# Dense products first at half clock, single turns, `pr` as one padded product, five last sums open in PSUM, and the last squares summed in three pieces

## The chip, the cores and the metric

The kernel runs on one core of a Trainium2 chip. The metric is the device time of one execution in microseconds (us). A core has TensorE (PE in the rows, PEld its weight loads), VectorE (DVE), ScalarE (ACT), GpSimd (POOL) and SyncE (SP), which here issues the transfers. The engines run their own instruction streams in order and wait for each other by semaphores.

## The reference

One layer of a hybrid decoder for a prompt of 1024 tokens and eight sample tokens that share the weights; width 1024, all in fp32:

```python
xn = _rms_norm(x, p['norm_g'][l])
h = xn @ p['w_in'][l]
pool_v, pool_g, rw, rw_g, q, xa_g = jnp.split(h, IN_SPLITS, axis=-1)
pool_y = _pool_mix(...) * jax.nn.silu(pool_g)
...
rws = rw + (prev - rw) * p['shift_mu'][l]
rwkv_y, S_T = _rwkv7(rws, wkv[l], ...)          # 8 heads of 64, a scan over the tokens
rwkv_y = rwkv_y.astype(x.dtype) * jax.nn.silu(rw_g)
xa_y = _cross_attend(q, mem_k[l], mem_v[l]) * jax.nn.silu(xa_g)
mixed = jnp.concatenate([pool_y, rwkv_y, xa_y], axis=-1)
x = x + mixed @ p['w_out'][l]
...
y = _rms_norm(x, p['final_norm_g'])
```

In `_rwkv7` the key is divided by its norm in each head (`kk / max(sqrt(sum(kk*kk)), 1e-12)`), and each token updates a 64 x 64 state per head.

## The kernel before

The activations lie with features on the partitions and tokens along the row. The prompt is worked in two parts: part 0 is 512 prompt tokens and the eight sample tokens (520 columns, two chunks of 260), part 1 is 512. Every fp32 operand of a large product is split into a high and a low half (type fp32r), and a product of one k-tile is three products: high x high, high x low, low x high. So an output tile of 128 features takes 24 products for eight k-tiles: `pt` in the input projection, `pto` in the output projection (`mh`, `ml`, `mu` are halves of its input).

The RWKV branch is cut into eight units (four pairs of heads x two parts). A unit goes through `rwkv_prep` (1124; the key norm is in it: sums of squares `pn` on PE, an rsqrt in nine small DVE operations `rsq_y`/`rsq_t`, ACT spreads it to `rsb`, PE multiplies it back as `prs`, DVE makes `kk`), then `rwkv_solve` (1269; inverts the small triangular blocks; the result is X), then `rwkv_solved` (1335; `pr` = X times C), then `rwkv_chain` (1348; `pc`, `py` with `Wd` between them, chunk after chunk) and `rwkv_norm` (1397). In `pr` the two heads of a unit take 64 rows each, so a group of four chunks is eight products of 64 x 64 tiles of PE.

The end of the program is `second_part` (1761): the output projection of part 1. Seven of eight k-tiles are summed for all eight output tiles first; each sum goes to SBUF with the residual `xres` added (DVE, `y`). When the last unit's k-tile (number 5) is there, three last products per tile follow (`w5`), DVE adds the tile (`y<-pto,y`), ACT squares it, DVE adds the square into `yacc`; the last tile's squares go to PE alone. `last_norm` (1804) sums `yacc` and `ysq` over the partitions on PE (`pss`), makes `ms` and its rsqrt, spreads it (`pb`), scales the tiles and stores `out_y`. `out_norm` (1854) does the same for part 0, in the middle of the output projection of part 1.

What sets the order is a planner in the program (`Loom`, 118): every operation is recorded (`record`, 223, called from line 228, which is why nearly all rows have that line) in a stream (chains, solves, preps, norms, fills, out_norm, samples and so on), and `weave` (452) plays the engines forward with estimated costs and emits each engine's sequence. Who goes first is decided by tables: RANK (45) gives each stream two priorities, one on PE and one on the other engines; LINE (54) is the order of work items (`k3` is the key tile of unit 3, `o1` the output projection of part 1, `g`, `v`, `r`, `p`, `h`, `x` others); HELP (62) says which small operations go to POOL or ACT instead of DVE. In `choose` (434) the next PE operation is picked: when the planner takes the clock to be half, operations whose estimated time is at most DENSE go last:

```python
return (cold and o.passes * o.cost <= DENSE, x[0][0] + (STAY if o.tiling != now else 0), x[0][1])
```

## Time and profile before

| | us |
|---|---|
| three executions | 704.91, 707.35, 1009.45 (median 707.35) |
| profiled execution | 701.2, its span 699.4 |
| PE busy | 645.4 (92%) |
| DVE busy | 532.3 (76%) |
| ACT busy | 433.2 (62%) |
| POOL busy | 161.9 (23%) |
| mean granted PE clock | 0.957 |

The span is the time from the first to the last instruction. A granted clock of 1.00 is 2.4 GHz, 0.50 is 1.2 GHz. In a row of the timeline stand the start, the duration of the group, the engine, the line, the operation, result <- operands, the shape and the number of instructions; in brackets the idle time of the engine ahead of it and what ended it. Durations of PE products overlap, so the step from one start to the next is the time that a product takes from the stream. An fp32 product (not fp32r) appears as two instructions.

### The profile page before, as it was taken

What the parts mean: (1) busy time and instruction counts of PE and PEld (TensorE: products, weight loads), DVE (VectorE), ACT (ScalarE), POOL (GpSimd) and SP (SyncE); (2) the same over time, 40 slices, a digit from 0 to 9 for tenths busy, and PEclk for the clock granted to TensorE, in tenths of its full rate; (3) what the DMA queues carried; (4) which work ended last, traced back from release to release, by engine and by line L of the source; (5) the groups of instructions that cost most, each with busy time, mean ns of one, the idle gap of its engine ahead of it and who ended that gap; (6) DMA issues with size and microseconds to landing.
All of it is one profiled execution on the core that took longest, in us unless ns stands there. A gap on an engine that the chain in (4) does not pass through costs nothing.

```text
span 699.4 us, 15473 instructions
## 1 busy us (share of the span) xinstructions
PE 645.4 (92%) x5698; PEld 559.6 (80%) x5698; DVE 532.3 (76%) x1318; ACT 433.2 (62%) x1233; POOL 161.9 (23%) x192
## 2 busy tenths in 40 slices
PE   8989999889999999999999889979989999998993
PEld 7989899778899878878788768767767888996762
DVE  7687789878886999688999496997675785557454
ACT  9487465658569577984465336555678987753221
POOL 3242523330421023231300040024021001221301
PEclk9999999989999999999899999999998999999995
DMA  7347468462342515225355725617404524657733
GB/s 253 115 143 257 145 234 286 156 207 76 111 170 91 197 62 165 67 83 191 88 174 170 262 90 160 236 48 219 128 14 141 176 85 152 220 168 243 237 114 120
DMA packets 59427, 109.40 MB, mean 156 GB/s; under 512 B 11144, under 2 KB 20432, under 8 KB 59352
## 3 DMA queue, kind: packets, MB, share of 16 engines
q1 hardware_dynamic: 59352, 108.42, 47.1%
q8 instruction: 45, 0.74, 0.4%
q14 instruction: 30, 0.25, 0.1%
HBM read 75.37 MB, written 33.02 MB: 155 GB/s over the span
## 4 chain that ended last, share of the span: by engine, by line
PE 50%; DVE 28%; DMA 8%; ACT 7%; issue 4%; SPq 1%; POOL 1%; DVEq 0%; ACTq 0%; POOLq 0%
PE pt L228 19%; PE pto L228 10%; PE pg L228 3%; PE py L228 3%; DMA w<-in_win 3%; PE pf L228 2%; DVE y L228 2%; DVE w L228 2%; DVE prod L228 2%; DVE Z L228 2%; DVE BK L228 1%; PE pr L228 1%; PE pc L228 1%; DMA Z<-in_zinit 1%; PE pkv L228 1%
## 5 line engine op out<-in xcount | busy, mean ns | idle before, releaser
L228 PE MATMUL pt<-xh,w 128*128 128x260 f32 (+1 forms) x1104 | 285.1, 339 | 4.6 <-DVE w L228 2.0
L228 PEld LDWEIGHTS pt<-xh,w 128*128 128x128 f32 x1104 | 188.7, 193 | 22.1 <-DVE w L228 2.8
L228 PE MATMUL pt<-xl,w 128*128 128x260 f32 (+1 forms) x552 | 185.3, 336 | 0.0
L228 PEld LDWEIGHTS pt<-xl,w 128*128 128x128 f32 x552 | 106.3, 193 | 7.8 <-issue 0.6
L228 PE MATMUL pto<-mh,w 128*128 128x260 f32 (+1 forms) x320 | 74.4, 313 | 2.3 <-DVE y L228 2.1
L228 DVE TENSOR_TENSOR w<-w,w 128x512 fp32r<-128x512 f32 x80 | 58.9, 743 | 21.9 <-ACT w L228 17.7
L228 ACT ACTIVATE w<-w 128x512 fp32r<-128x512 f32 x96 | 58.3, 623 | 24.7 <-DMA w<-in_win 13.3
L228 PEld LDWEIGHTS pto<-mh,w 128*128 128x128 f32 x320 | 52.7, 189 | 8.1 <-DVE y L228 5.4
L228 PE MATMUL pto<-ml,w 128*128 128x260 f32 (+1 forms) x160 | 50.3, 314 | 0.0
L228 POOL TENSOR_TENSOR w<-w,w 128x512 fp32r<-128x512 f32 x16 | 26.7, 1667 | 80.8 <-ACT w L228 63.0
L228 ACT ACTIVATE SV<-py,PC 64x64 f32<-64x64 f32 x112 | 34.7, 309 | 17.1 <-PE py L228 15.3
L228 PE MATMUL py<-SV,E 128*128 128x64 f32 x256 | 38.2, 266 | 0.0
L228 PEld LDWEIGHTS py<-SV,E 128*128 128x128 f32 x256 | 35.6, 196 | 1.7 <-ACT Y L228 0.5
L228 ACT ACTIVATE Wd<-pc 64x64 f32<-64x64 f32 x128 | 27.7, 216 | 14.9 <-PE pc L228 13.2
L228 PE MATMUL pg<-E,BK 64*128 64x128 f32 x256 | 32.6, 304 | 3.7 <-DVE BK L228 3.1
L228 PEld LDWEIGHTS pg<-E,BK 64*128 64x128 f32 x256 | 27.5, 205 | 9.5 <-POOL BK L228 2.3
L228 PEld LDWEIGHTS pto<-ml,w 128*128 128x128 f32 x160 | 30.2, 189 | 1.1
L228 PE MATMUL pc<-SV,E 128*128 128x128 f32 x128 | 27.1, 294 | 3.5 <-ACT SV L228 3.3
L228 ACT ACTIVATE LX<-pg 32x256 f32<-32x256 f32 x64 | 20.5, 321 | 15.7 <-PE pg L228 14.5
L228 PE MATMUL pto<-mu,w 128*128 128x512 f32 x96 | 26.5, 420 | 2.3 <-DVE w L228 2.3
L228 PE MATMUL py<-Wd,C 128*128 128x128 f32 x128 | 27.2, 295 | 1.5 <-ACT Wd L228 1.5
L228 DVE TENSOR_TENSOR y<-pto,xres 128x260 f32<-128x260 f32 (+1 forms) x24 | 12.1, 511 | 21.4 <-PE pto L228 20.9
(354 smaller groups left out, 1442.6 us busy)
## 6 DMA issues: line engine op xcount, KB each, us to landing
w<-in_win SPq DMA_DIRECT2D x98, 256.0 KB, 3.7
ws<-w SPq DMA_DIRECT2D x34, 512.0 KB, 3.8
w<-ws SPq DMA_DIRECT2D x34, 512.0 KB, 4.0
out_y<-y SPq DMA_DIRECT2D x16, 256.0 KB, 2.1
xr<-in_xT SPq DMA_DIRECT2D x12, 256.0 KB, 3.3
xr<-in_xT SPq DMA_DIRECT2D x8, 260.0 KB, 4.4
mr<-mixd SPq DMA_DIRECT2D x8, 260.0 KB, 2.6
xres<-in_xT SPq DMA_DIRECT2D x8, 260.0 KB, 3.6
```

Of the source, the lines that this page charges most:

```text
L228: op = Op(eng, lambda: f(*a, **k), (x[1] if eng == "PE" else x[2], self.seq))
```

## The change

- The planner's tables: RANK has new numbers, LINE another order. The rule in `choose` now puts last the operations whose columns are at most 0.7 of their estimated time (RICH) when the planner takes the clock to be half; DENSE is not read any more. A new table NUDGE moves 238 single operations (named by stream and number) up or down in priority.
- A second queue of transfers on ACT (`out`, `aq`), and other engines for three operations of the chain (`helped("wm")` and so on): HELP names none of them, so nothing goes there. HELP names one new entry, `xr1`.
- `pr`: X is written into a lasting tile XB of 128 x 128 blocks whose off-diagonal quarters are zeroed once at the start. A group is four products with 128 rows instead of eight with 64; sixteen memsets of X go.
- `second_part`: output tiles 3 to 7 keep their sums in five PSUM banks. Their residual is split in two halves (`xr`, ACT and POOL) and added by two products with an identity (`identr`). The last products go on summing there. Tiles 0 to 2 are taken out and added as before. `w5` comes in four transfers at output tile 4. Squares read PSUM. The sums over partitions are twelve products of three pieces: `yacc` of tiles 0 to 5, then the squares of tile 6, then of tile 7.
- `last_norm`: tiles 3 to 7 are scaled out of PSUM into new tiles.

PE has 4232 products instead of 4282 (`pr` 64 instead of 128, `pss` with `ysq` 8 instead of 4, ten identity products); DVE has 11 operations fewer, ACT 6 more, POOL 10 fewer.

```diff
-LINE = ("v0 k3 o0 r3 x r6 g0 k1 v3 r4 k2 h1 p3 k4 k5 g1 r1 v5 g6 v1 k6 v6 p1 v2 v7 r5 k7 o1 r2 v4 p0 g7 h0 g3 "
-        "p2 g4 g5 r7 g2")
-DENSE = 112.0
+LINE = ("v0 k3 o0 r3 r6 k1 v3 p3 r4 k2 g0 h1 x g1 k4 k5 r1 g6 v5 v1 v2 v6 k6 p1 v7 r2 r5 o1 k7 p2 h0 v4 p0 g7 "
+        "g3 g4 g5 r7 g2")
+RICH = 0.7
+NUDGE = {
+    ('ahead_of_chain', 1, 151): -0.1, ('ahead_of_chain', 1, 158): -0.1, ('ahead_of_chain', 1, 159): 67.2,
...
+        key = (*x[7], n)
+        turn = (x[1] if eng == "PE" else x[2]) + NUDGE.get(key, 0.0)
...
-                return (cold and o.passes * o.cost <= DENSE, x[0][0] + (STAY if o.tiling != now else 0), x[0][1])
+                return (cold and o.columns <= RICH * o.passes * o.cost, x[0][0] + (STAY if o.tiling != now else 0), x[0][1])
...
-            po.memset(X[r1, :, 32:64], 0.0)
+            X = XB[:, :, r1.start:r1.start + 64]
...
-            for hr in (LO, HI):
-                pe.matmul(pr_[hr, 128 * c:128 * c + 128], X[hr, 4 * g + c, :], C[hr, c, :],
-                          start=True, stop=True)
+            pe.matmul(pr_[:, 128 * c:128 * c + 128], XB[:, 4 * g + c, :], C[:, c, :], start=True, stop=True)
...
+            if ft == 4:
+                w5 = []
+                for q in range(4):
...
+                    sy.dma_start(w5[q].bitcast(F32), wlast[:, 2 * q:2 * q + 2])
...
+            o = mmb("pto") if ft < 5 else fill("pto") if ft == 5 else sol("pto") if ft == 6 else wide("pto")
+            if ft >= 3:
+                xr = [rp.tile([P, HT], F32R, tag=t_, name="xr" + t_) for t_ in ("u4", "u5")]
+                split(xres, *xr, vp("xr", 1))
...
-            ve.tensor_tensor(y, o, xres, op=ALU.add)
-            Y.append(y)
+            if ft >= 3:
+                for x in xr:
+                    pe.matmul(o, identr, x, start=False, stop=False)
+                Y.append(o)
...
-            ve.tensor_tensor(y, o, y, op=ALU.add)
+            if ft < 3:
+                ve.tensor_tensor(y, o, y, op=ALU.add)
...
+            for j in range(4 if ft >= KT - 3 else 0):
+                pe.matmul(pss[:, j:j + 1], (acc if ft == KT - 3 else sq)[:, 128 * j:128 * j + 128], ones_c,
+                          start=(ft == KT - 3 and j == 0), stop=(ft == KT - 1 and j == 3))
...
-                ve.scalar_tensor_tensor(y, y, col(C_FG, ft), pb, op0=ALU.mult, op1=ALU.mult)
+                ve.scalar_tensor_tensor(y, o, col(C_FG, ft), pb if ft < 3 else rsy, op0=ALU.mult, op1=ALU.mult)
```

**Place A: PE, the last products.** Rows of the instruction order (line, operation, result <- operands, columns; the numbers behind a name are buffers). Before, `w_1505` is the last k-tile's weight, `mh_1493` and `ml_1494` its input; the sums over the partitions follow in pairs:

```order
L228 MATMUL pto<-ml_1494,w_1505 128x512
L228 MATMUL pto<-mh_1493,w_1505 128x512 x2
L228 MATMUL pto<-ml_1494,w_1505 128x512
L228 MATMUL pto<-mh_1493,w_1505 128x512
L228 MATMUL pss<-ones_c,yacc 128x1
L228 MATMUL pss<-ones_c,ysq 128x1
L228 MATMUL pss<-ones_c,yacc 128x1
L228 MATMUL pss<-ones_c,ysq 128x1
L228 MATMUL pss<-ones_c,yacc 128x1
L228 MATMUL pss<-ones_c,ysq 128x1
L228 MATMUL pss<-ones_c,yacc 128x1
```

After, with `w_1485` and `w_1486` two of the four pieces of that weight and `xru` the halves of a residual:

```order
L317 MATMUL pto<-mh_1498,w_1485 128x512
L317 MATMUL pto<-xru_1509,identr 128x512
L317 MATMUL pto<-xru_1510,identr 128x512
L317 MATMUL pto<-ml_1499,w_1485 128x512
L317 MATMUL pto<-mh_1498,w_1485 128x512 x2
L317 MATMUL pto<-ml_1499,w_1485 128x512
L317 MATMUL pto<-mh_1498,w_1485 128x512
L317 MATMUL pto<-mh_1498,w_1486 128x512
L317 MATMUL pto<-ml_1499,w_1486 128x512
L317 MATMUL pto<-mh_1498,w_1486 128x512 x2
L317 MATMUL pto<-ml_1499,w_1486 128x512
L317 MATMUL pto<-mh_1498,w_1486 128x512
```

Right behind them on PE, after (`pb` spreads the scale over the partitions):

```order
L317 MATMUL pss<-ones_c,yacc 128x1 x4
L317 MATMUL pss<-ones_c,ysq 128x1 x8
L317 MATMUL pb_1526<-con,rsq_y 128x128 x3
L317 MATMUL pb<-con,rsq_y 128x128 x4
L317 MATMUL pb_1526<-con,rsq_y 128x128
```

Two identity products stand among the last 24 products, and `pss` is four products of `yacc` and then eight of squares in one row.

**Place B: DVE and SP, out_norm of part 0** (`y<-y,cols,rsx` is the scaling of an output tile, `w_1464<-w_1465,w_1464` the low half of a weight that PE waits for). DVE before:

```order
L228 COPY Y<-py 64x2x64 x4
L228 TENSOR_REDUCE gsm<-Y 128x8
L228 TENSOR_TENSOR y<-pto,xres 128x512
L228 SCALAR_TENSOR_TENSOR y<-y,cols,rsx 128x520 x8
L228 TENSOR_TENSOR w_1464<-w_1465,w_1464 128x4x128
L228 TENSOR_TENSOR y<-pto,xres 128x512
```

DVE after:

```order
L317 TENSOR_TENSOR y<-pto,xres 128x512
L317 SCALAR_TENSOR_TENSOR y<-y,cols,rsx 128x520 x7
L317 TENSOR_TENSOR w_1456<-w_1457,w_1456 128x4x128
L317 TENSOR_TENSOR y<-pto,xres 128x512
L317 SCALAR_TENSOR_TENSOR y<-y,cols,rsx 128x520
L317 COPY Y<-py 64x2x64 x4
L317 TENSOR_REDUCE gsm<-Y 128x8
L317 TENSOR_SCALAR gsm<-gsm 128x8
L317 TENSOR_TENSOR w_1464<-w_1465,w_1464 128x4x128
L317 TENSOR_TENSOR y<-pto,xres 128x512
```

A weight split now stands ahead of the last scaling, and the next one (`w_1464`) behind the copies of Y. SP before (`w<-in_win` is a raw weight coming in):

```order
L228 DMA w_1465<-in_win 128x512
L228 DMA w_1466<-in_win 128x512
L228 DMA xres<-in_xT 128x512
L228 DMA out_y<-y 128x512
L228 DMA out_y<-y 128x8
L228 DMA out_y<-y 128x512
```

SP before, at the end of the sixteen `out_y`:

```order
L228 DMA out_y<-y 128x8
L228 DMA out_y<-y 128x512
L228 DMA out_y<-y 128x8
L228 DMA w_1474<-in_win 128x512
L228 DMA w_1475<-in_win 128x512
```

SP after:

```order
L317 DMA w_1457<-in_win 128x512
L317 DMA w_1458<-in_win 128x512
L317 DMA xres<-in_xT 128x512
L317 DMA out_y<-y 128x512
L317 DMA out_y<-y 128x8
```

SP after, at the end of the `out_y`:

```order
L317 DMA out_y<-y 128x512
L317 DMA out_y<-y 128x8
L317 DMA w_1465<-in_win 128x512
L317 DMA out_y<-y 128x512
L317 DMA out_y<-y 128x8
L317 DMA out_wkvp<-Sf_144 128x64
L317 DMA w_1466<-in_win 128x512
```

The raw weight that was issued after all sixteen `out_y` is issued after fourteen.

**Place C: DVE, the key norm of the seventh unit** (`ss<-pn` begins the rsqrt; `th` is a scan of 1.2 us; `Kt`, `sc` belong to the sample tokens, `Y<-py` to the norm of another unit, `prod` and `Z` to the next solve). Before:

```order
L228 SCALAR_TENSOR_TENSOR pv_1034<-ppool,hps,g_1059 128x512
L228 STREAM_TRANSPOSE XN<-XD 128x256
L228 TENSOR_TENSOR Kt<-Kt,qb 128x512 x2
L228 TENSOR_REDUCE sc<-Kt 128x8 x2
L228 COPY Y<-py 64x2x64 x4
L228 SCALAR_TENSOR_TENSOR th<-smask,th 128x512
L228 TENSOR_REDUCE gsm<-Y 128x8
L228 TENSOR_SCALAR ss<-pn 128x8
L228 TENSOR_SCALAR gsm<-gsm 128x8
L228 TENSOR_SCALAR rsq_y<-ss 128x8
L228 TENSOR_TENSOR rsq_t<-rsq_y 128x8
```

After:

```order
L317 SCALAR_TENSOR_TENSOR th<-smask,th 128x512
L317 TENSOR_TENSOR qhl<-q,qhl 64x256 x2
L317 TENSOR_TENSOR prod<-Ls,Z 128x24
L317 SCALAR_TENSOR_TENSOR g_1093<-g_1093,pt_0_1095 128x512
L317 TENSOR_TENSOR Z<-Z,prod 128x2x4x3
L317 TENSOR_TENSOR Y<-Y,rsq_y 128x512
L317 TENSOR_REDUCE mx<-psc 128x2
L317 TENSOR_TENSOR prod<-Ls,Z 128x16
L317 TENSOR_SCALAR ss<-pn 128x8
L317 TENSOR_SCALAR mx<-mx 128x2
L317 TENSOR_TENSOR Z<-Z,prod 128x2x4x2
L317 TENSOR_SCALAR rsq_y<-ss 128x8
```

`Kt`, `sc` and the copies of Y no longer stand ahead of the scan and of `ss`; small steps of a solve stand between the steps of the rsqrt. At the sixth unit, PE before, from `pn` to `prs`:

```order
L228 MATMUL pn<-con,sq 128x2 x4
L228 MATMUL pt_0_990<-xh_708,w_975 128x512
L228 MATMUL pt_0_990<-xl_709,w_975 128x512
L228 MATMUL pt_0_990<-xh_708,w_975 128x512
L228 MATMUL pt_0_990<-xh_711,w_975 128x512
L228 MATMUL pt_0_990<-xl_712,w_975 128x512
```

PE after:

```order
L317 MATMUL pn<-con,sq 128x2 x4
L317 MATMUL pt_0_990<-xh_708,w_973 128x512
L317 MATMUL pt_0_990<-xl_709,w_973 128x512
L317 MATMUL pms<-ys,bmaskr 128x32
L317 MATMUL pt_0_990<-xh_708,w_973 128x512
L317 MATMUL pt_0_990<-xh_712,w_973 128x512
L317 MATMUL pt_0_990<-xl_713,w_973 128x512
L317 MATMUL pv<-low,XD 32x16 x32
L317 MATMUL prs<-con,rsb 128x128 x4
L317 MATMUL pt_0_990<-xh_712,w_973 128x512
```

Sixteen products stood between `pn` and `prs` there (six rows of the pattern are shown); now there are five, with `pms` and `pv`.

## Rows read from the trace of the kernel before

**Rows 1.** The page's head and busy time, share and count by engine.
```profile
span 699.4 us, 15473 instructions
...
PE 645.4 (92%) x5698; PEld 559.6 (80%) x5698; DVE 532.3 (76%) x1318; ACT 433.2 (62%) x1233; POOL 161.9 (23%) x192
```
**Rows 2.** Stretches at half clock: length, busy time by engine, PEclk, DMA share, GB/s.
```profile
469.10:472.50 3.40, 3.40 (x23) 2.23 (x11) 3.40 (x8) 0.00 (x0) 2.61 (x3) 0.50 0.00 0
...
643.18:646.58 3.40, 3.40 (x9) 2.65 (x8) 0.19 (x3) 2.02 (x16) 1.04 (x1) 0.50 0.73 226
684.14:699.42 15.28, 5.16 (x24) 4.68 (x23) 5.51 (x15) 1.67 (x3) 2.49 (x2) 0.50 0.37 137
sum 59.55, PE 47.51 PEld 40.69 DVE 39.70 ACT 22.68 POOL 11.32; mean PE 4.32 PEld 3.70 DVE 3.61 ACT 2.06 POOL 1.03
```
**Rows 3.** PE's waits by cause: us in total, times, longest.
```profile
PE prs L228 <- ACT rsb L228: 5.2, 3, 3.8
...
PE pto L228 <- DVE w L228: 2.3, 1, 2.3
```
**Rows 4.** Timeline of PE around one `pr` group.
```profile
600.02 0.28 PE L228 MATMUL pto<-mh,w 128*128 128x260 f32 x1
600.24 1.09 PE L228 MATMUL pr<-C,X 64*64 64x128 f32 x16
601.25 0.39 PE L228 MATMUL pto<-mh,w 128*128 128x260 f32 x1
```
**Rows 5.** The page's costliest groups: POOL's splits, busy and mean ns.
```profile
L228 POOL TENSOR_TENSOR w<-w,w 128x512 fp32r<-128x512 f32 x16 | 26.7, 1667 | 80.8 <-ACT w L228 63.0
```
**Rows 6.** The chain of work that ended last: start, us, what.
```profile
619.47 0.22 PE pc L228 x2
...
629.65 0.91 PE pss L228 x10
...
653.40 20.62 PE pto L228 x89
...
683.18 0.69 DVE yacc L228
...
683.92 3.43 PE pss L228 x16
...
687.37 0.17 DVE ms L228
```
**Rows 7.** Timeline of the end: the first last product, the last square.
```profile
674.30 0.98 PE L228 MATMUL pto<-mh,w 128*128 128x512 f32 x2
...
683.36 0.63 ACT L228 ACTIVATE ysq<-y 128x512 f32<-128x512 f32 x1 [0.57 <-DVE y L228]
```
**Rows 8.** Timeline of DVE and of SP's queue at part 0's out_norm.
```profile
635.50 6.49 DVE L228 SCALAR_TENSOR_TENSOR y<-y,cols,rsx 128x520 f32<-128x520 f32 x8
641.91 0.68 DVE L228 TENSOR_TENSOR w<-w,w 128x512 fp32r<-128x512 f32 x1
...
636.27 8.79 SPq L228 DMA_DIRECT2D out_y<-y  x16
```
**Rows 9.** Timeline of PE, then DVE, at the seventh unit's key norm.
```profile
458.08 1.05 PE L228 MATMUL pn<-con,sq 128*128 128x2 f32 x8
...
467.92 0.66 PE L228 MATMUL prs<-con,rsb 128*128 128x128 f32 x4 [3.84 <-ACT rsb L228]
...
462.35 0.16 DVE L228 TENSOR_SCALAR ss<-pn 128x8 f32<-128x8 f32 x1
...
465.92 1.23 DVE L228 SCALAR_TENSOR_TENSOR rsq_y<-rsq_t,rsq_y 128x8 f32<-128x8 f32 x1
```
**Rows 10.** Timeline of PE and ACT at the sixth unit's key norm.
```profile
395.98 1.05 PE L228 MATMUL pn<-con,sq 128*128 128x2 f32 x8 [1.88 <-DVE bz L228]
...
398.94 0.63 ACT L228 ACTIVATE rsb<-rsq_y 128x512 f32<-128x512 f32 x1 [3.78 <-DVE rsq_y L228]
```

More of the change, by code (lines that the diff above doesn't have):

```diff
@@ L54 @@
-LINE = ("v0 k3 o0 r3 x r6 g0 k1 v3 r4 k2 h1 p3 k4 k5 g1 r1 v5 g6 v1 k6 v6 p1 v2 v7 r5 k7 o1 r2 v4 p0 g7 h0 g3 "
-        "p2 g4 g5 r7 g2")
-DENSE = 112.0
+    "last_norm": (-1.5, -2.8), "start": (10.9, -34.6), "norm_x": (-42.1, 50.2), "later": (-8.9, 40.9), "chains":
+    (14.6, -16.3), "ahead_of_chain": (5.1, -83.0), "solves": (7.4, -9.3), "preps": (1.6, 113.4), "norms":
+    (-25.1, 21.2), "out_norm": (-12.8, -32.1), "pool_rest": (14.0, -36.7), "attention": (5.9, -33.7), "samples":
+    (8.5, 13.0), "second_mixed": (20.9, -49.6), "memory": (-33.9, -27.0), "fills": (20.7, 15.1), "second_stats":
@@ L80 @@
     __slots__ = ("eng", "call", "cost", "turn", "left", "after", "ready", "start", "end", "tiles", "bytes", "tiling",
-                 "spot", "passes", "columns", "port", "watch", "lane")
+                 "spot", "passes", "columns", "port", "watch", "lane", "key")
     def __init__(self, eng, call, turn):
@@ L227, in record @@
         outs = [aps[0]] + ([k["accum_out"]] if "accum_out" in k else [])
-        op = Op(eng, lambda: f(*a, **k), (x[1] if eng == "PE" else x[2], self.seq))
+        self.order[x[7]] = n = self.order.get(x[7], 0) + 1
+        key = (*x[7], n)
+        turn = (x[1] if eng == "PE" else x[2]) + NUDGE.get(key, 0.0)
+        op = Op(eng, lambda: f(*a, **k), (turn, self.seq))
+        op.key = key
         if eng == "PE":
@@ L301, in begin @@
             op.end, self.free["PE"] = end + 185, end - work + min(work, 20)
-        elif op.eng == "DMA":
-            self.free["DMA"] = self.t + op.cost
+        elif op.eng in ("DMA", "OUT"):
+            self.free["DMA" if op.eng == "DMA" else "ACT"] = self.t + op.cost
             self.ring = max(self.ring, op.start + 1800) + op.bytes / 270
@@ L350, in mark @@
         for key in keys:
-            self.marks[key] = [o for o in self.cur[5] + self.cur[6] if o.eng != "DMA" and (o.end is None or o.end > self.t)]
+            self.marks[key] = [o for o in self.cur[5] + self.cur[6] if o.eng not in ("DMA", "OUT") and (o.end is None or o.end > self.t)]
             for x in self.unmarked.pop(key, ()):
@@ L423, in step @@
         if w is END:
-            ops = [o for o in x[5] if o.eng != "DMA"]
+            ops = [o for o in x[5] if o.eng not in ("DMA", "OUT")]
             x[3] = f = lambda: False
@@ L468, in weave @@
                         heapq.heappush(q, (turn, op))
-                    if q and self.free[e] <= self.t:
+                    if q and self.free["ACT" if e == "OUT" else e] <= self.t:
                         self.begin(self.choose(e, q))
@@ L553, in trunk @@
     bmask = bmaskr.bitcast(F32)
+    identr = cp.tile([P, 128], F32R, tag="identr", name="identr")
     ones_c = cp.tile([P, 1], F32, tag="ones_c", name="ones_c")
@@ L584, in trunk @@
     EA = (slice(128, 192), slice(0, 64))
+    XB = cp.tile([P, 8, 128], F32, tag="XB", name="XB")
     Wd = [cp.tile([P, 128], F32, tag=f"Wd{b}", name=f"Wd{b}") for b in range(2)]
@@ L591, in vp, with out @@
         return po if helped(what, pt) else ve
+    def out(what, pt=0):
+        return aq if helped(what, pt) else sy
     def half_c(name, dt=F32):
@@ L1291, in rwkv_solve @@
         ve.transpose(XD.rearrange("p c (a g) -> p a g c", g=4), Z)
-        X = rp.tile([P, 8, 64], F32, tag="X", name="X")
         XN = rp.tile([P, 8, 32], F32, tag="Z", name="XN")
@@ L1801, in second_part, with last_norm @@
                 ac.activation(sq, y, AF.Square)
-        loom.add(last_norm(Y, acc, sq))
-    def last_norm(Y, acc, sq):
+            if ft == KT - 3:
+                pss = ps_c.tile([P, 512], F32, tag="chain", name="pss")
+            for j in range(4 if ft >= KT - 3 else 0):
+                pe.matmul(pss[:, j:j + 1], (acc if ft == KT - 3 else sq)[:, 128 * j:128 * j + 128], ones_c,
+                          start=(ft == KT - 3 and j == 0), stop=(ft == KT - 1 and j == 3))
+        loom.add(last_norm(Y, pss))
+    def last_norm(Y, pss):
+        ms = sp.tile([P, 4], F32, tag="ms4", name="ms")
+        ve.tensor_scalar(ms, pss[:, 0:4], 1.0 / D, EPS, op0=ALU.mult, op1=ALU.add)
+        rs = rsqrt(ms, 4, sp)
         yield END
-        rs = rstd(acc, HT, more=sq)
-        yield END
-        pb, pc = fill("pb"), sol("pb2")
+        pb, pc = ps_y.tile([P, 512], F32, tag="py", name="pb"), wide("pb2")
         for b in (pb, pc):
@@ L1997, in start @@
             ve.memset(W, 0.0)
+        po.memset(XB, 0.0)
         warm = sol("warm")
```

193 lines of the change are left out of this document (144 added, 49 removed).

## The prediction

> **What bounds the kernel now.** The head of the profile's page [rows 1] comes first: TensorE (PE) is busy 645.4 of 699.4 us, the vector engine (DVE) 532, ScalarE (ACT) 433, GpSimd (POOL) 162. PE is short of the span by 54.0 us. The clock row and then the table of the stretches at half clock [rows 2] say where the clock fell: to 1.2 GHz (0.50) in eleven stretches of 59.55 us together. The last, 684.14 to 699.42, is the end of the kernel and holds 15.28 - 5.16 = 10.1 us of PE's idle time. So before 684 PE stands idle for 43.9 us and works at half clock for 44.3 us, which costs at most half of that, 22.1 us. Those 66 us are the pot for a new order; whatever cuts PE's own work pays in full, because PE hardly ever has spare time. The table of PE's waits [rows 3] names the largest: 5.2 us before `prs` (the key norm sent back over the rows), 2.3 us before `pto` (an output tile waiting for a split weight). The rest are many waits of about a microsecond.
>
> The end is different. There PE waits for DVE: the chain of waits [rows 6] runs through `yacc` on DVE, then sixteen `pss` passes at half clock, then `ms`. What shortens the end there must shorten DVE's row of adds.
>
> **1. The padded product.** A `pr` group today is eight 64x64 products, sixteen passes in the trace. From the start of the last `pto` product ahead (600.02) to the first `pto` product behind (601.25) there are 1.23 us [rows 4]; a 260-wide `pto` product itself steps 0.12, so a group takes 1.12 us with its entry. Its replacement is four 128x128 products, and there is a product of exactly that shape in the kernel: `pc` steps 0.22 us for its two passes [rows 6]. Four take 0.88. The gain is 0.24 us a group, 16 groups, **-3.8 us**. The lower bound of gain is 0, where PE waits right behind for ACT's copy of `pr` anyway; the upper is -5, where some groups stand in half-clock time. The sixteen POOL memsets of X go, one memset at the start comes; POOL is busy 23% [rows 1], nothing on PE waits for it here, so 0. `XB` is one buffer for all units where X was taken anew: the writes of a unit wait for the `pr` of the unit before. Solves of neighbouring units lie tens of microseconds apart, so 0; if they came to overlap, a unit's `pr` would be late by up to one group, 1 us.
>
> The Trainium skill speaks against this edit: "TensorEngine Tiling (Array Packing)", in its table of theoretical speedup, promises up to 2x from packing a contraction of 64 or less, which the old form does and the new one gives up. It also says, under the key properties, that changing the mode drains the engine. With its factor of two the new group would cost 2 x 1.0 us instead of 0.88, +16 us in all; the `pc` row disagrees, and the sum goes by the row.
>
> **2. The five open sums and the squares in three pieces.** Today, from the last products' start (674.30) to `ms` (687.37) are 13.07 us [rows 6, 7]. Within, DVE makes eight `y` adds and six `yacc` adds, 0.69 each one after the other, 9.7 us in all; then `pss` starts at 683.92 and takes 3.43 us for sixteen passes, 0.214 each, at half clock. At full clock ten passes take 0.91, at most 0.11 each with what is around them [rows 6]. After: the order (places A and B ahead) puts 24 products and two identity products in that stretch, and a 512-wide product steps 20.62/89 = 0.232 us [rows 6], so PE is through at 6.0 us. DVE has only three `y` adds and five `yacc` adds, 5.5 us, in PE's shade. ACT squares the eighth tile 0.63 us [rows 7] after its last product, at about 6.9, when PE has already summed `yacc` and begins on the seventh tile's squares. PE has 24 passes of `pss`: 2.6 us at 0.11, so `ms` starts near 8.9. That is -4.2. If the clock falls first, 24 x 0.214 = 5.1 and `ms` starts at 11.3: -1.7. I take **-4.1**, since PE no longer pauses between the products as it does now. The other eight identity products lie ahead of the stretch: 8 x 0.23 = **+1.8**. Five residual splits more go to ACT and POOL. POOL's 128x512 split takes 1.67 us on average [rows 5]; an output tile takes PE some 5 us (21 products), so it is hidden; without that cover the first identity product would wait up to 1.7 us. The last scaling reads PSUM instead of SBUF on DVE, six operations as before; 0. What follows `ms`, 12.0 us to the end, stays.
>
> **3. The stall at the first part's out_norm.** DVE scales eight y tiles of 520 columns in one row, 6.49 us, and behind it stands the weight split that PE needs at 639.9: the wait of 2.3 us [rows 3, 8]. On SyncE (SP) the sixteen `out_y` issues take 8.79 us [rows 8], and the next raw weights are issued behind them. In the new order (place B) the split `w_1456` stands after seven of eight scalings, and the issue of raw `w_1465` stands after 14 `out_y` issues. So the first wait shrinks by one scaling of 0.81, and the next weight arrives with SP still 14/16 x 8.79 = 7.7 us busy. I count the stall as moved by one tile and slightly smaller, **-0.6**. Bounds: 0, and -2.3 - 1.7 = -4.0 if it goes with the half-clock stretch at 643.18 [rows 2].
>
> **4. The key norms.** At the seventh unit `pn` starts at 458.08, but DVE reads it only at 462.35, behind the scores of the sample tokens, copies of Y and a scan, and the rsqrt ends at 465.92 + 1.23; PE waits 3.84 us and starts `prs` at 467.92, 9.8 us after `pn` [rows 9]. The clock falls at 469.10 [rows 2]. In the new order (place C) `Kt`, `sc` and the Y copies no longer stand ahead of that scan and rsqrt. With a free DVE the same chain is short: at the sixth unit `pn` starts at 395.98 and ACT is through with `rsb` at 398.94 + 0.63, 3.6 us [rows 10]. So the wait goes, 3.84, with half of 3.4 us of half clock, 1.7: -5.5. In exchange the new order puts less PE work between `pn` and `prs` at the fifth and sixth units. At the sixth stand five products and two small groups, about 2.0 us where the chain after `pn` needs 3.1; at the fifth about 2.7 against 3.6. That is 1.1 + 0.9, and one half-clock stretch more, 1.7: +3.7. Net **-1.8**; bounds -5.5 and +3.7.
>
> **5. All the rest of the order.** The first 130 us keep nearly their order; from there to 620 the weave is new in hundreds of places, with the rule on dense products and the table of single turns. No row of before prices that. The pot is the 66 us above, less what 3 and 4 name. The products between the steps of the chain (`pc`, `py`) are about as many as before, so I take 0, with -13 (a fifth of the pot) and +10 for the bounds.
>
> The sum: -3.8 - 4.1 + 1.8 - 0.6 - 1.8 = -8.5 us. The profiled execution took 701.2 us (its span of 699.4 and 1.8 around it) and would take 692.7. The runs shown are 704.9 and 707.35, the median (a third, 1009, is no like of theirs); the profiled one is 0.9% under that median. I put the forecast on the middle of the three, 704.9: **696.4 us**, its own range 692 to 701. Under 2% (below 690.8 or above 719.0) a measurement of this kernel can hardly tell from no change.
>
> **The rivals.** *A, the new order frees more.* A dense stretch that keeps the clock up saves twice, the wait and the half clock behind it. A sixth of the pot, 11 us, gives 685. For it: the waits are small and many, the kind that single turns remove, and each half stretch follows such waits. Against: the rows of the order show new short covers beside the longer ones. *B, nothing comes through.* The gain at `pr` turns into a wait for ACT's copy, the end runs at half clock (-1.7), and the eight identity products cost 1.8: 704, in 701 to 709. For it: chains of small steps, not PE's work, may set the middle. Against: PE is 92% busy. *C, the key norms get worse.* If at the fifth and sixth units DVE's queue is as loaded as at the seventh today (from the end of `pn`, 458.08 + 1.05, to `prs` 8.8 us), covers of 2.3 and 1.6 leave waits of 6.5 and 7.2, and 3.4 to 6.8 us of half-clock cost with them: 17.1 to 20.5 in place of the 3.7 counted, so +5 to +8 in all, 710 to 713. It decides from the point where DVE reads `pn` more than 5 us late at both. Against it: place C's order shows the rsqrt interleaved with short solve steps, not behind long ones. *D, the padded product is dear.* If a 128x128 product with half its weights zero costs what two packed groups do, a group takes 2 us and the kernel 717. Against it stands `pc`'s row, whose operands are padded in the same way. D is what the Trainium skill's page on tiling would have.
>
> **Chances.** The forecast 0.42, A 0.35, B 0.14, C 0.07, D 0.02. 683 to 709 leaves out the far side of A (about 0.08) and C and D (0.09). Faster by over 2%: A and a little of the forecast, 0.37. Slower by over 2%: D and the top of C, 0.04. The rest, 0.59, lies between.
>
> **What would show it.** Step 1: `pr` groups of eight passes at 0.88 us in the timeline. Step 2: no `y<-pto,y` on DVE for five tiles, `pss` of 24 passes right behind the products, `ms` 8.9 us after the first last product. Step 3: a PE wait for `w` near out_norm of about 1.9. Step 4: no PE wait over 1 us for `rsb` at the seventh unit, about 1 at the fifth and sixth. Step 5: PE's idle time before the end at 40 to 44 us and half clock at about 44. It would be wrong above all if step 5 is not 0: then the idle time and the half-clock stretches between 130 and 630 us move by more than 10 us together.

## The result, and the profile after

The changed kernel took 697.16 us (median of four executions, 692.84 to 699.17), the kernel before 706.13 (704.91 without its execution of 1009.45); the ratio is 0.989, its 95% interval 0.985 to 0.9935. That is the forecast to within a microsecond (696.4), inside its range, and within 2%. Twelve more executions of the same file later gave 0.997 (0.993 to 1.0003). Executions of one kernel lie up to 13 us apart here, and part of that goes with the mean granted clock of PE, so four are few: over all, the changed kernel has a mean of 698.9 us (16 executions) and the kernel before of 703.0 (95, all of the later sessions). The change is worth about 4 us (+-2), 0.6%; the predicted sum of 8.5 is twice that. By session the means differ by 8.9 us (four against three executions) and by 2.7 (twelve against 23): that the first comparison met the forecast so closely is in part luck. The ratios leave out executions more than 1.5% over the fastest of their kernel; the means leave out only three of over 1000 us.

| | before | after |
|---|---|---|
| profiled execution, its span | 701.2, 699.4 | 696.43, 694.7 |
| PE busy to `ms` | 643.4 of 687.4 | 643.8 of 682.5 |
| PE idle to `ms` | 44.0 | 38.8 |
| half clock to `ms`, as recorded | 47.6 | 41.1 |
| `ms` to the end | 12.05 | 12.15 |

PE's busy time up to `ms` comes from the table of stretches (length, then busy time of PE, PEld, DVE, ACT and POOL, PEclk, DMA share, GB/s). The kernel before:

```profile
0.00:687.37 687.37, 643.42 (x5690) 558.05 (x5690) 526.83 (x1303) 432.64 (x1232) 159.39 (x190) 0.97 0.48 156
```

The changed kernel, with its nine recorded half-clock stretches (the first seven of them, which answer to [rows 2], and the sum):

```profile
0.00:682.51 682.51, 643.75 (x5580) 564.75 (x5580) 514.99 (x1292) 435.03 (x1238) 160.32 (x180) 0.97 0.48 157
```

```profile
126.05:129.46 3.41, 3.41 (x43) 3.11 (x43) 3.38 (x8) 2.18 (x6) 2.73 (x4) 0.50 0.36 125
143.12:146.53 3.41, 3.41 (x18) 3.41 (x18) 3.40 (x6) 1.67 (x5) 1.85 (x2) 0.50 0.97 391
149.94:156.77 6.83, 6.83 (x32) 6.49 (x31) 3.64 (x8) 2.04 (x8) 0.00 (x0) 0.50 0.33 87
180.66:187.49 6.83, 6.83 (x34) 6.83 (x33) 4.82 (x26) 1.77 (x7) 0.00 (x0) 0.50 0.31 123
197.73:204.56 6.83, 6.69 (x52) 5.45 (x53) 6.10 (x15) 1.58 (x5) 2.63 (x2) 0.50 0.49 167
344.50:351.33 6.83, 4.80 (x25) 4.39 (x26) 4.63 (x9) 2.47 (x8) 0.00 (x0) 0.50 0.42 131
487.86:491.27 3.41, 3.41 (x19) 2.28 (x19) 3.32 (x6) 1.43 (x5) 1.76 (x2) 0.50 0.00 0
...
sum 53.20, PE 40.55 PEld 36.54 DVE 36.91 ACT 16.19 POOL 11.48; mean PE 4.51 PEld 4.06 DVE 4.10 ACT 1.80 POOL 1.28
```

What to see: the whole gain of the profiled execution, 4.7 us, is idle time of PE (5.2 less); PE's busy time is the same. The stretches at 469 and 643 [rows 2] are gone, others have come at 126, 181 and 198.

The clock's record doesn't begin with the span: in this trace its first entry is at 13.4 us, in the one of before at 4.9. PE's timeline of the changed kernel shows what is missing:

```profile
11.57 0.42 PE L317 MATMUL pf<-xl,w 128*128 128x260 f32 x1
11.79 0.64 PE L317 MATMUL pf<-xh,w 128*128 128x260 f32 x2
...
13.48 0.28 PE L317 MATMUL pf<-xl,w 128*128 128x260 f32 x1
13.60 0.40 PE L317 MATMUL pf<-xh,w 128*128 128x260 f32 x2
```

A 260-wide product steps 0.22 us (11.57 to 11.79) from the first at 5.9 up to 13.3 and 0.12 (13.48 to 13.60) behind: some 7 us at half clock that no row counts. With them the changed kernel has 48 us of half clock up to `ms`, no less than before, and its mean clock of 0.962 is 0.005 too high.

PE's waits of the changed kernel (total us, times, longest), against [rows 3]:

```profile
PE px L317 <- ACT LX L317: 3.7, 3, 1.9
PE pg L317 <- DVE BK L317: 3.1, 2, 2.2
...
PE prs L317 <- ACT rsb L317: 1.4, 3, 0.7
...
PE pto L317 <- ACT w L317: 1.1, 1, 1.1
```

The wait for `rsb` fell from 5.2 to 1.4 and the one for a split weight is 1.1; a wait of the solves (`px`), which was not among the large ones, is now the largest. Not all of it comes back in other executions: the longest `px` wait, 1.9 us at 198, is 0 and 0.1 in the two other traces of this order (the changed kernel again, and with two queues), while both have a wait of 1.5 us for `rsb` that this one lacks, and 2.9 for `rsb` in all:

```profile
189.52 0.65 PE L317 MATMUL prs<-con,rsb 128*128 128x128 f32 x4 [1.52 <-ACT rsb L317]
```

### The profile page after: what moved, and what is told of

It reads as the page before. It is cut to its first block, busy times and chain, and to the rows that moved or that the text cites. A ratio compares the mean times of both kernels' runs of the same rounds, so it can differ in the third digit from the quotient of the medians.

```text
span 694.7 us, 15234 instructions
## 1 busy us (share of the span) xinstructions
PE 645.7 (93%) x5588; PEld 566.3 (82%) x5588; DVE 520.5 (75%) x1307; ACT 435.6 (63%) x1239; POOL 162.8 (23%) x182
## 5 line engine op out<-in xcount | busy, mean ns | idle before, releaser
L317 POOL TENSOR_TENSOR w<-w,w 128x512 fp32r<-128x512 f32 x16 | 23.8, 1489 | 100.9 <-ACT w L317 74.6
L317 ACT ACTIVATE LX<-pg 32x256 f32<-32x256 f32 (+1 forms) x64 | 20.5, 321 | 21.7 <-PE pg L317 20.6
L317 DVE TENSOR_TENSOR E<-pg,con 64x512 f32<-64x512 f32 x32 | 22.0, 687 | 12.2 <-ACT LX L317 11.8
L317 PEld LDWEIGHTS pc<-SV,E 128*128 128x128 f32 x128 | 21.3, 193 | 8.5 <-ACT SV L317 4.7
L317 DVE TENSOR_TENSOR raw<-pt,rsx 128x260 f32<-128x260 f32 x36 | 15.1, 423 | 16.4 <-PE pt L317 16.3
```

The source lines that it names most:

```text
L317: op = Op(eng, lambda: f(*a, **k), (turn, self.seq))
```

## The experiments

Many kernels here keep the order of another one row for row on every engine: the planner records and plans the old operation, and another is emitted in its place. So a part can be changed alone. Where the planner weaves anew, it is said.

| kernel | executions | mean us | mean clock | ratio to before (95%) |
|---|---|---|---|---|
| before | 95 | 703.0 | 0.960 | |
| after, all | 16 | 698.9 | 0.954 | |
| padded `pr` in before's order | 11 | 700.6 | 0.958 | 0.997 (0.994 to 0.9996) |
| all structure in before's order | 12 | 699.4 | 0.959 | 0.994 (0.991 to 0.997) |
| after with 64x64 `pr` | 12 | 704.5 | 0.953 | 1.002 (0.9996 to 1.005) |
| after with closed sums | 12 | 702.2 | 0.949 | 0.9997 (0.997 to 1.003) |
| after, two queues at the end | 12 | 698.6 | 0.955 | 0.9955 (0.992 to 0.999) |
| after without single turns | 6 | 712.4 | 0.957 | 1.015 (1.009 to 1.020) |
| after with the old rule | 6 | 722.5 | 0.935 | 1.028 (1.0235 to 1.0325) |
| structure with before's tables, woven anew | 4 | 730.6 | 0.940 | 1.040 (1.034 to 1.046) |
| before with short scores | 10 | 701.1 | 0.962 | 0.998 (0.9955 to 1.001) |
| after with waits filled | 12 | 697.8 | 0.963 | 0.992 (0.989 to 0.995) |
| after with more waits filled | 10 | 697.0 | 0.9635 | 0.984 (0.980 to 0.988) |

Within one kernel, over all these executions, 0.01 more of mean clock goes with 3.6 us less (one slope fitted to all kernels, each with its own level; 1.9 us are left over). "At one clock" below means the mean moved along this slope to 0.957. It is an estimate: the record of the clock begins 4.6 to 13.7 us into the span in the traces kept, and a half-clock start that it misses moves one execution's mean clock by up to 0.005. The kernels of this table were run in four sessions (four executions of the changed kernel in an earlier one), in which the mean of the kernel before lay between 702.4 and 704.4.

### Padded products in the order of before

```diff
-                pe.matmul(pr_[hr, ...], X[hr, 4 * g + c, :], C[hr, c, :], start=True, stop=True)   # two per chunk
+                pe.eng.matmul(pr_[:, ...], XB[:, 4 * g + c, :], C[:, c, :], start=True, stop=True)  # emitted once, in their place
```

> The kernel before with its own order kept on every engine, row for row; only the sixteen pr groups are four padded 128x128 products each instead of eight 64x64 ones. Theory 1 (PE's work pays in full): the trace of the changed kernel shows a group at 0.81 us where it was 1.02 and shows no 0.095 us of entry, so 16 x 0.30 = 4.8 us less, a ratio of 0.993. Rival B (the gain becomes a wait for the copy of pr): under 1 us, ratio 0.999 to 1.000. Rival D (padding costs double): +16 us, ratio 1.023.

Measured: 0.997, 700.6 us against 702.8 in the same session, -2.2; at one clock -3.3 (+-0.6). Its trace is of an execution of 2056 us and gives no rows; the kernel of all structure, below, has the same order and the same groups. There and in the kernel before, fourteen groups run at full clock, and group by group, with the entry and without waits, the padded ones are 0.03 to 0.37 us shorter, 3.2 in sum. Theory 1 in kind, its size less than said; clearly not rival D.

### The changed kernel with 64x64 products again

```diff
+            def halves(c=c):
+                for r in (LO, HI):
+                    pe.eng.matmul(pr_[r, 128 * c:128 * c + 128], XB[r, 4 * g + c, r], C[r, c, :], start=True, stop=True)
+            loom.ops[-1].call = halves
```

> The changed kernel with its order kept on every engine; only each pr group is again eight 64x64 products, read from the diagonal quarters of XB. Theory 1: 16 x 0.30 = 4.8 us slower than the changed kernel, ratio to the kernel before 0.996. Rival B: no slower than the changed kernel, 0.989.

Measured: 704.5 us, 5.6 over the changed kernel's 698.9; at one clock 5.2. Theory 1. PE's timeline of the changed kernel around one group:

```profile
553.87 0.39 PE L317 MATMUL pto<-mh,w 128*128 128x260 f32 x1
554.10 1.10 PE L317 MATMUL pr<-C,XB 128*128 128x128 f32 x8
554.95 0.37 PE L317 MATMUL pto<-ml,w 128*128 128x260 f32 x1
```

and of this kernel, at its nearest group:

```profile
554.77 0.39 PE L317 MATMUL pto<-mh,w 128*128 128x260 f32 x1
555.09 1.09 PE L1443 MATMUL pr<-C,XB 64*64 64x128 f32 x16
556.11 0.39 PE L317 MATMUL pto<-ml,w 128*128 128x260 f32 x1
```

From the product ahead to the product behind: 1.08 us padded, 1.34 packed, 0.26 less here (one `pto` product ahead in both). In the changed kernel's groups at full clock the eight passes step 0.81 to 0.99 us from their first to the next product, 0.81 at best and 0.98 where `pg` (64 rows) follows; the sixteen packed ones step 1.02 whatever follows, behind an entry of 0.1. Group by group that is 0.02 to 0.33 us, 3.0 in sum for the fourteen at full clock; the two at half clock add 0.4 to 1.4, depending on the trace. The runs show 5.2 +- 0.7: what is beyond the rows stays open.

### All structure in the order of before

The two edits of `pr` and `second_part` (open sums, identity products, three pieces) in the kernel before, its order kept up to the last output tiles; tables and rule stay.

```diff
+        XB = cp.tile([P, 8, 128], F32, tag="XB", name="XB")        # and padded pr as above
-    def second_part():  ...  def last_norm(Y, acc, sq):  ...       # of before
+    def second_part():  ...  def last_norm(Y, pss):  ...           # of the changed kernel
-        "... wl11 xs1 ..."
+        "... wl11 xr1 xs1 ..."
```

> The kernel before with its own order kept up to the last output tiles, and all structural parts of the change: padded pr, five open sums with identity products, squares in three pieces. What is missing of the change is the tables and the rule alone. From the changed kernel's trace: pr -4.8, the end -3.3 (9.8 us from the first last product to ms instead of 13.1), identity products ahead of the end +1.8. Theory (the parts add up): -6.3 us, ratio 0.991, and the tables are then worth what is left of the whole change's 0.989, about 1 to 2 us. Rival (the new order carries the change): ratio 0.996 or more, and the tables are worth 5 us. Second rival (the order costs): ratio under 0.989.

Measured: 0.994, 699.4 us, -3.4 in its session; at one clock -4.0. Between the theory and the first rival. What is left for the tables is 0.5 us as it stands and 2.5 at one clock. The end of it on PE:

```profile
684.26 0.40 PE L228 MATMUL pto<-mh,w 128*128 128x512 f32 x1
685.82 1.05 PE L228 MATMUL pss<-ones_c,yacc 128*128 128x1 f32 x8 [1.16 <-DVE yacc L228]
686.74 1.93 PE L228 MATMUL pss<-ones_c,ysq 128*128 128x1 f32 x16
```

`pss` runs at full clock and waits 1.16 us for DVE's last `yacc`. And the stall at out_norm is there as in [rows 3], 2.33 us up to 645.25, but no half clock behind it in this execution: the stall alone doesn't bring the stretch at 643 [rows 2].

### The changed kernel with the old end

```diff
-    def second_part():  ...  def last_norm(Y, pss):  ...           # of the changed kernel
+    def second_part():  ...  def last_norm(Y, acc, sq):  ...       # of before
```

> The changed kernel with its order kept up to the last output tiles, and from there the end of the kernel before: all eight sums taken out with the residual on DVE, last products added on DVE, squares in one sum and one piece. Theory 2: the stretch from the first last product to ms is 13 us again instead of 9.8, and eight identity products (1.8 us) are gone ahead of it: 1.5 us slower than the changed kernel, ratio to the kernel before 0.991. Rival: the identity products and the splits eat the gain, ratio 0.989 or below. Second rival: the DVE adds of residuals, now gone, had held up more than the end: 4 us slower, ratio 0.995.

Measured: 702.2 us, 3.3 over the changed kernel; at one clock 1.7. The theory (1.5), though as it stands the second rival can't be ruled out: its mean clock is 0.949. The end of the changed kernel, in the chain of work:

```profile
674.31 0.69 DVE y L317
...
675.70 0.70 DVE yacc L317
...
678.89 0.70 DVE yacc L317
...
679.63 2.85 PE pss L317 x24
...
682.51 0.17 DVE ms L317
```

From the first last product (672.72) to `ms` are 9.79 us. With the old end in the same order they are 12.33, from 674.55 to

```profile
684.63 2.23 PE pss L317 x16
686.88 0.17 DVE ms L317
```

and not 13.53 as in the kernel before: the sixteen `pss` passes take 2.2 us here at mostly full clock, and 3.43 there at half clock [rows 6]. So 1.2 us of the difference to before is the clock, and 2.5 the new end. ACT shows what paces DVE there:

```profile
677.28 0.60 ACT L317 ACTIVATE ysq<-pto 128x512 f32<-128x512 f32 x1 [0.20 <-DVE yacc L317]
678.08 0.60 ACT L317 ACTIVATE ysq<-pto 128x512 f32<-128x512 f32 x1 [0.20 <-DVE yacc L317]
```

A tile's square waits for the add of the tile two ahead, which frees its buffer, and its own add waits for the square: 0.69 for the add, 0.60 for the square and 0.30 between them make 1.59 us for two tiles, 0.80 for one, where the adds alone would take 0.69. DVE also begins only 0.89 us after the first last product (673.61), so its three `y` adds and five `yacc` adds would not quite fit under PE's products even at 0.69. `pss` waits 0.71 us for the last one.

### The changed kernel again, and four variants of its tables and its end

> The changed kernel once more, unaltered, with more executions and on the same chip as the others of this call: executions of one and the same kernel lie up to 9 us apart here, and four of each gave a ratio of 0.989 in 0.985 to 0.9935. If the parts measured so far (padded pr -2, all structure -3 to -4 in the order of before) are the change, the ratio is 0.993 to 0.995; if the new order adds to them, 0.985 to 0.990.

Measured: 0.997, 699.7 us in twelve executions. So the first ratio was on the good side, and the parts are the change: what the new order adds is small. At one clock the two parts taken out of the changed kernel cost 5.2 and 1.7, as much together as the whole change is worth (6.5), so by these runs the new order without them would stand where the kernel before does.

Without single turns (`NUDGE = {}`, woven anew):

> The changed kernel without the table of single turns (238 operations keep the priority of their stream); all else as in the changed kernel, so the planner weaves anew wherever a turn had moved something (805 rows of difference on PE). Theory (the turns each take away a wait): 5 us or more slower than the changed kernel. Rival (the gain is in the parts and the tables of streams and items): within 2 us of it.

Measured: 1.015, 13.5 us over the changed kernel, at a clock no lower: the theory's size. PE is idle for 694.98 - 642.15 = 52.8 us up to `ms`, 14 more than with them:

```profile
0.00:694.98 694.98, 642.15 (x5580) 560.49 (x5580) 519.57 (x1292) 434.96 (x1238) 156.41 (x180) 0.98 0.46 154
```

The weave is another one in 805 rows, and its other tables were made together with the turns: what the turns are worth one by one isn't shown.

With the old rule (woven anew):

```diff
-                return (cold and o.columns <= RICH * o.passes * o.cost, ...)
+                return (cold and o.passes * o.cost <= 112.0, ...)
```

> The changed kernel with the old rule in choose (operations of at most 112 of estimated time go last when the planner takes the clock to be half), all other tables as in the changed kernel, so the weave is new (900 rows of difference on PE). If putting dense products first keeps the clock up: more half-clock time before the end than the changed kernel's 41 us, and 3 us or more slower. Rival: the rule only picks another weave, and the time is within 2 us either way.

Measured: 1.028, 23.6 us over the changed kernel; idle 47.1 us, and the busy time is 21 us longer, since PE stands at half clock for 89 us ahead of the end by the record, against 41:

```profile
0.00:712.12 712.12, 665.03 (x5580) 580.10 (x5580) 525.13 (x1292) 435.43 (x1238) 159.57 (x180) 0.94 0.46 151
```

The theory on the clock is borne out in this weave. But this kernel has turns that were made for another weave, so the rule's own worth isn't told apart from that.

Two queues at the end (`HELP` names `Qy1`):

> The changed kernel with its order kept; only four of the last eight stores go out by the queue on ACT (HELP names Qy1) instead of all eight by SP. In the changed kernel's trace DVE ends its last scaling at 690.15 and SP issues its last store from about 690.9 on, 0.42 us each. Theory: SP's issues are the last thing behind DVE, 0.8 to 1.2 us faster than the changed kernel. Rival: the landing of the last store sets the end, whatever queue issues it: 0.

Measured: 698.6 us against 698.9, at one clock 0.2 over it: the rival. The last store is issued by ACT, and no earlier behind DVE's last scaling (ended 687.54) than by SP: its issue ends at 688.74, 1.20 us behind, and in the changed kernel it is 1.20 too:

```profile
686.13 1.41 DVE L317 SCALAR_TENSOR_TENSOR yo<-pto,cols,rsx 128x512 f32<-128x512 f32 x2
```

```profile
686.24 0.38 ACTq L317 DMA_DIRECT2D out_y<-y  x1
686.90 1.84 ACTq L317 DMA_DIRECT2D out_y<-yo  x3
```

From `ms` to the end are 12.16 us, 12.14 in the changed kernel.

### The structure with the tables of before, woven anew

The edit, by the names of the tables alone:

```diff
-RANK, LINE, NUDGE, RICH rule of the changed kernel
+RANK, LINE, DENSE rule of the kernel before, NUDGE = {}
```

> The changed kernel with all the tables and the rule of the kernel before (streams, items, DENSE at 112, no single turns); the planner weaves anew, since the padded products and the open sums change its costs (865 rows of difference on PE against the kernel before, from row 762 on). The same parts in the kernel before's own order, row for row, gave a ratio of 0.994. Theory (a weave that no table was made for costs, as without the turns): 5 us or more slower than with the order kept, ratio 1.002 to 1.02. Rival (the weave is robust, the parts decide): 0.992 to 0.997.

Measured: 1.040, 730.6 us: 31 us over the same parts with the order kept. PE is idle for 56.4 us up to `ms` and at half clock for 68 us ahead of it:

```profile
0.00:712.95 712.95, 656.50 (x5580) 572.85 (x5580) 524.27 (x1293) 435.36 (x1238) 162.32 (x180) 0.95 0.45 150
```

I had not reckoned with this: other products give the planner other ready times, the weave differs from row 762 of PE on, and the tables, made for the old weave, seem to fit no longer (that a weave no table was made for is dear is also what the two kernels above show; no run tells which table it was). The new tables of the change win little over the old order (0.5 to 2.5 us); they win back the 30 us that the new parts would have cost under the old tables.

### Short scores ahead of the seventh key norm

```diff
+                if bh == 3:    # planned as before, emitted on 8 columns
+                    loom.ops[-1].call = lambda ...: ve.eng.tensor_tensor(Kt[:, 0:8], Kt[:, 0:8], qb[:, 0:8], op=ALU.mult)
```

> The kernel before with its order kept; the four DVE operations (Kt twice, sc twice) of the last pair of sample heads, which stand ahead of the scan and of ss<-pn at the seventh unit's key norm, work on a few columns instead of 512 (the scores of these heads are not the reference's). That takes about 1.9 us of DVE's queue away. Theory 4 (DVE's queue makes PE's wait of 3.84 us at prs): the wait falls to about 1.9 and the kernel by 1.9 us, by 3.6 if the half-clock stretch behind it goes too: ratio 0.995 to 0.997. Rival (the scan or ACT's rsb ends the wait): the wait stays near 3.8 and the time the same.

Measured: 0.998 (0.9955 to 1.001), 701.1 us, -1.8 in its session, -1.4 at one clock, hardly clear of noise. The wait at `prs` is 3.08 us where it was 3.84 [rows 9], between the theory's 1.9 and the rival's 3.8:

```profile
469.98 1.12 PE L228 MATMUL prs<-con,rsb 128*128 128x128 f32 x4 [3.08 <-ACT rsb L228]
```

DVE's timeline shows where the rest of the 1.9 us went:

```profile
459.92 0.25 DVE L1704 TENSOR_REDUCE sc<-Kt 128x8 f32<-128x16 f32 x2
461.46 1.20 DVE L228 COPY Y<-py 64x128 f32<-64x128 f32 x4 [1.30 <-ACT Sf L228]
462.69 1.23 DVE L228 TENSOR_TENSOR_SCAN th<-smask,th 128x512 f32<-128x512 f32 x1
...
464.41 0.16 DVE L228 TENSOR_SCALAR ss<-pn 128x8 f32<-128x8 f32 x1
```

The copies of Y, next in DVE's queue, wait 1.30 us for ACT, and the scan and `ss` stand behind them. By these rows both the scores and the copies have to leave their places, as they do in the change, to free the norm; the copies were not moved alone.

### Waits filled with zero products

In the changed kernel's order, a product is repeated with zero weights where PE waits; nothing is computed by it.

```diff
+        if n in FILL[kind] and not k["stop"]:
+            for _ in range(FILL[kind][n]):
+                self.pe.eng.matmul(a[0], self.zer, a[2], start=False, stop=False)
```

> The changed kernel with its order kept; in 25 places where three traces of it show PE waiting 0.3 us or more behind a pt or pto product, that product is repeated with zero weights (fp32r, the same columns, added to the open sum, so the result stays) as often as fits into the shortest of the three waits: some 90 products, 12 us of work in waits. Theory (the half clock comes from the waits, the waits from other engines): the places keep their time, half-clock time before the end falls from 41 to 48 us to under 30, the mean granted clock rises above 0.965 and the time falls by 4 us or more. Rival (the half clock comes from the stretches of small products, the solves and the key norms, not from the waits): the clock stays at 0.95 to 0.96 and the time within 2 us. Second rival: the repeats delay what stands behind them; slower by up to 5 us.

Measured: 0.992, 697.8 us, 1.1 under the changed kernel; the mean clock rises from 0.954 to 0.963. One place, before and after filling:

```profile
598.99 0.28 PE L317 MATMUL pto<-ml,w 128*128 128x260 f32 x1
600.24 0.34 PE L317 MATMUL px<-LX,XD 32*32 32x32 f32 x10 [0.96 <-ACT LX L317]
```

```profile
604.52 0.28 PE L325 MATMUL pto<-ml,w 128*128 128x260 f32 x1
604.63 1.12 PE L565 MATMUL pto<-ml,zer 128*128 128x260 f32 x8
605.73 0.69 PE L325 MATMUL px<-LX,XD 32*32 32x32 f32 x32
```

The step from the `pto` product to `px` was 1.25 us and is 1.21 with eight more products in it. So this wait was one for another engine, and the mean clock rises with what PE does in such waits. But the half clock ahead of the end did not fall under 30 us (47.8 by the record of the profiled execution), and the time gains less than the clock's slope promises (3.5 us): in time it is the rival. The last kernel fills 34 places:

> The changed kernel with its order kept, as in after_filled, but 34 places and 126 products with zero weights (17.5 us of work in waits): also behind small products, into whichever sum stands open; the three places where after_filled made PE late are left out. Where after_filled kept each place's time within 0.02 us, the time of the places does not move here either. Theory (waits make the half clock, and after_filled raised the mean clock from 0.954 to 0.963): the clock rises to 0.965 or more and the time falls by 3 to 5 us against the changed kernel's pooled mean, ratio to the kernel before 0.987 to 0.991. Rival (what was left at half clock are stretches of small products, which no filled wait reaches): clock and time as in after_filled, ratio 0.992 to 0.994. Second rival (changes of tile shape around the products inside small work cost more than the waits hold): slower than after_filled, ratio over 0.995.

Measured: 697.0 us in ten executions, against 704.4 of the kernel before in fifteen, 0.990 (the table's 0.984 is of five of the ten). The clock is the same 0.963 as with 25 places, as the rival has it; the ratio of the means lies where the theory put it, but the time is only 1.9 us under the changed kernel's pooled mean where 3 to 5 were said. So neither is settled. PE is idle for 22.9 us up to `ms`, 16 less than the changed kernel, since the zero products count as busy, and the stretch from 479 to 496 stays at half clock in it as from 487 to 504 with fewer filled:

```profile
484.00:505.00 21.00, 20.87 (x126) 17.17 (x126) 10.99 (x22) 8.84 (x25) 4.52 (x5) 0.59 0.27 94
```

(This row is of the kernel with 25 places.) PE is busy there with hardly a pause, with products of the attention, the samples, a solve and the input projection. The filled kernels have the lowest means of all, 1 to 2 us under the changed kernel, but that is not clear of the scatter (each mean is uncertain by about 1 us).

## Why the prediction was right, and where it was not

The total came out, and several of its terms did not; they made up for one another.

**1, the padded product.** -3.8 forecast; 3.3 (+-0.6) in the old order, 5.2 (+-0.7) in the new, both at one clock. Right, with the mechanism: PE has little spare time, so the product's time is nearly the kernel's. The padded group was put at 0.88 us from `pc`'s step and measured 0.81 to 0.99, the packed one at 1.12 with its entry, as it is; the mean gain of a group at full clock, 0.22 us, is nearer to the forecast's 0.24 than to the 0.30 of the later expectations.

**2, the end.** -4.1 for the stretch to `ms`, +1.8 for identity products. The stretch went from 13.53 to 9.79, -3.7 (the first last product of before starts at 673.84; I had taken 674.30, the third). Of these 3.7, 1.2 are the clock under `pss`. The failing step is "in PE's shade": DVE begins 0.89 us late, ACT's square and DVE's add wait for each other, 0.80 us a tile, and `pss` waits 0.71 us for `yacc`. Net -1.7 (+-0.7) at one clock where -2.3 was said.

**3, out_norm.** -0.6 forecast as a moved stall. It is 1.1 us, now for ACT's `w` at 644.63, so -1.2; right in kind. The bound that took the half clock with it has no support: the kernel of all structure has the stall without that stretch.

**4, the key norms.** -1.8 net forecast. The seventh unit's wait is gone, as said. The step that failed is the price of the short covers: 1.1 and 0.9 us and a half-clock stretch were counted for the fifth and sixth unit, and the rows show 0.29 and 0.42 (the steps from the product ahead are 0.46 and 0.49 too long), and no half clock begins right behind them. So all waits for `rsb` fell by 3.8 us in this execution, and by 2.3 in the second trace, where one of 1.5 us at 189.5 is added.

```profile
335.48 0.65 PE L317 MATMUL prs<-con,rsb 128*128 128x128 f32 x4 [0.29 <-ACT rsb L317]
...
419.49 0.66 PE L317 MATMUL prs<-con,rsb 128*128 128x128 f32 x4 [0.42 <-ACT rsb L317]
```

**5, all the rest.** Taken as 0. PE's idle time up to `ms` fell by 5.2 us in all. Terms 3 and 4 make 5.0 of it, and the end another 3.4, by these rows of before

```profile
PE pto L228 <- DVE y L228: 2.1, 6, 0.7
PE pss L228 <- DVE yacc L228: 2.0, 1, 2.0
```

and 0.7 for `yacc` after: so elsewhere about 3 us of waits were added in this execution. The half clock did not fall, with the start counted. And the new order makes PE's own products dearer. Summed from start to start without the waits, and half-clock steps counted half (an estimate from the traces), they take 620.6 us up to `ms` before, 617.8 with all structure in the order of before, and 620.9 to 621.8 in three traces of the new order, while the waits fall from 46.3 to between 37.8 and 39.9: the new order buys some 7 us of waits with some 3 us of steps. In the mean clock the change loses too, 0.960 to 0.954 over all executions, some 2.4 us by the slope. This is the term that was mis-sized: what the runs leave for it beside the other four is +3 to +5 at one clock, and the 2.4 of the clock on top, not 0. It took back what 1, 3 and 4 gave beyond the forecast and, over many executions, half of the sum. The sign that the prediction named for it, idle and half-clock time between 130 and 630 us moving by more than 10 us together, did not show (30.0 to 27.7 idle, 34.1 to 37.6 at half clock): dearer steps were not in it.

The rivals: A (a better order) didn't come, B (nothing comes through) is further off than the forecast in the first comparison and about as near over all executions (-0.9 and -8.5 against -4.1), C and D did not happen. On the rule of the Trainium skill behind D ("TensorEngine Tiling (Array Packing)", theoretical speedup, up to 2x): packing two contractions of 64 gained nothing here; the packed group took 1.12 us with its entry, the padded one 0.81 to 0.99. One packed pass is the shorter one, 1.02/16 = 0.064 us against 0.81/8 = 0.10, but there are twice as many. The entry of 0.095 us behind a product of another shape agrees with the drain on a change of mode that the Trainium skill names on the same page under the key properties.

## What to carry to other kernels

Where an engine is busy 92% of the time, what its own instructions save is nearly the kernel's gain; a filler in its waits cost nothing in the place shown, and a shorter instruction was mostly not swallowed by them. But where a planner sets the order, each structural part must be measured with the order kept: the same parts gave 0.994 that way and 1.040 when the planner wove anew with tables made for the old costs. A small block padded to the full array can beat the packed form when the packed form needs twice the passes and a change of shape. And before half-clock time is compared between two traces, look where the record of the clock begins.

## What the runs showed of the hardware

- In a fixed order some of PE's waits repeat to 0.01 us and others don't: the step from the last `pt` product to `pr` near 270 was 1.009, 1.007 and 1.007 us in three traces, but `prs` near 190 waited 0, 1.52 and 1.52. Of 55 waits that reach 0.3 us in one of the three, 22 repeat to 0.02 and ten differ by over 0.5. Executions of the changed kernel differ by 11 us and their granted clock by 0.943 to 0.964; why a stretch falls in one and not in the next is left open.
- The record of the granted clock begins 4.6 to 13.7 us into the span, and its sums can miss a half-clock start: 260-wide products step 0.22 us there and 0.12 later. The step tells the clock where the record doesn't.
- Sixteen passes of 64x64 products step 1.02 us, eight of 128x128 over the same data 0.81 to 0.99, the most where `pg` or `ppool` follows.
- A half-clock stretch can stand where PE is busy with hardly a pause (487 to 504, above), so idle time inside it alone does not keep it up.
